# Sample keys of a head pair in one tile, memory weights and mix rows loaded earlier, the memory keys' root on GpSimd

## The chip, the cores and the metric

The kernel runs on one core of a Trainium2 chip. The metric is device time in microseconds of one execution. TensorE (PE in the profile) multiplies and transposes, VectorE (DVE) and ScalarE (ACT) evict, cast and normalize, GpSimd (POOL) does elementwise work on SBUF, and SyncE (SP) issues the DMAs.

## The reference

One layer of a streaming encoder is computed for a prompt of 1024 rows and a sample of 64 rows (width 1024). Both go through an RMS norm, a combined projection to queries, keys and values, and two groups of 8 heads of 64: group A attends in a chunk band with a learned bias, group B causally with a forget gate. Then come the output projection, cross-attention into 256 memory tokens (4 heads of 256), and a gated feed-forward block with a causal convolution of width 3.

What the change touches:

```python
# memory: keys and values of the 256 memory rows
kv = rms_norm(mem, g_mem) @ w_mkv
k = rms_norm(kv[..., :D_MODEL].reshape(b, n, H_M, HEAD_DIM_M), g_mk)
v = kv[..., D_MODEL:].reshape(b, n, H_M, HEAD_DIM_M)
# sample: 64 queries per head against cached keys (A 512, B 1024 rows) and its own 64
k = jnp.concatenate([cache_k, ka], axis=1)
v = jnp.concatenate([cache_v, va], axis=1)
logits = jnp.einsum('bqhd,bkhd->bhqk', q, k) * scale + bias
```

Inputs are fp32, and the outputs also include the new keys and values.

## The kernel before, in words

Every fp32 factor is split into a rounded high part and the remainder (`hi`, `lo`, type fp32r), and a product is the sum of three: high x high, high x low, low x high (`SPLIT`). Where two parts are stacked over the 128 partitions, one matmul does two of them at once.

The program has a phase of projections with the prompt's attention (`Attn`), then the stage around the change, then the output projection (`gemm`, L937), cross-attention and the feed-forward block.

The stage around the change interleaves two kinds of work.

- The memory: 16 units (n, t), n being one of 8 column groups of 256 of `w_mkv` (0 to 3 are keys, 4 to 7 values) and t one of 2 row blocks. A unit is four pieces of six matmuls (`mem_piece`, L679), summed into one of the two buffers of the PSUM bank `pj`. `load_wm` fetches half of a group's weights (512 KB), `split_wm` splits a quarter: ACT casts the high part (L668), GpSimd or DVE subtracts (L669). `mem_end` evicts a unit: for keys the squares' sum (L695), the root of the mean (`rsq`: logarithm and exponential on ACT, three steps on DVE), and the scaled copy `kv` (L698); for values a scaled copy on ACT (L701). `mem_turn` transposes a key unit on PE (L710) and stores it.
- The sample: 8 pairs of heads (`Sample`, in the order `SAMPLES`: four of group B, then four of A). `load` fetches the rows of the pair; `prep` transposes queries and new keys (L754) and splits them into `sq` and `skn`; `splitk` splits the cached keys into `kchi` (ACT, L774) and `kclo` (DVE, L775); `score` multiplies 512 keys at a time (wide products, L797) and the 64 new ones (narrow products, L798), evicts with the running minimum (L800, L802) and takes the exponential on ACT (L808); `turn` transposes the weights (L822) and evicts them as `pth` (ACT) and `ptl` (DVE); `sum` multiplies with the values (L835) and combines the halves (`st` on ACT L842, `su` on DVE L843); `out` transposes (L847) and copies to `smix` (ACT L849).

Before the change each head's keys lie twice in the 128 partitions, against a query tile with the high part above and the low part below, and with zeros in the columns of the other head. So a chunk of 512 keys takes four wide products: two heads, each with `kchi` and `kclo`.

The pieces of the memory are in the list `line`. 15 of them are woven into the last steps of the prompt's attention (`LEFT`), the others into the samples' steps in portions of `PER`. The mix rows (the prompt's attention output, 8 tiles of 128 x 1024) come back from DRAM when `line` is used up: `open_left` loads four, and `split_mix` splits each into `a` (ACT L979, DVE L980); they are the moving operand of the output projection, whose first weights are cast by ACT (L919) and subtracted on GpSimd (L920).

The program gives a list of steps; a scheduler in the framework then sets the order of each engine's queue by its own model of times. Each queue runs in order, so an instruction that waits holds all those behind it.

Of the kernel before, what the change touches and what calls it, by code (L numbers as in the profile page):

```python
# [28 lines left out]
STAGE, MIXES = 4, 8  # L29
# [12 lines left out]
def hybrid_step(ctx: ExitStack, tc: tile.TileContext, i: dict, o: dict):  # L42
# [23 lines left out]
    sqk = dram.tile([8, S, 512], F32, name="sqk")  # L66
# [275 lines left out]
    def proj_sample(p, subs):  # L342
# [22 lines left out]
        def store():  # L365
# [5 lines left out]
            nc.sync.dma_start(sqk[p], qk[:S].rearrange("p h a d -> p (h a d)"))  # L371
# [287 lines left out]
    def load_wm(n, z):  # L659
        raw = mp.tile([P, 4, 256], F32, name="mwraw", bufs=2)  # L660
        nc.sync.dma_start(raw.rearrange("p k c -> p (k c)"), i["w_mkv"][n, z])
        wraw[n, z] = raw

    def split_wm(n, y):
        raw = wraw[n, y // 2][:, 2 * (y % 2):2 * (y % 2) + 2]
        hi = mp.tile([P, 2, 256], F32R, name="mwhi", bufs=6)
        lo = mp.tile([P, 2, 256], F32R, name="mwlo", bufs=6)
# [17 lines left out]
    def mem_end(n, t):  # L685
        pj = mpj.pop((n, t))[:, :256]
        kv = mp.tile([P, 256], F32, name="kv", bufs=2)
# [3 lines left out]
        if n < 4:  # L691
# [4 lines left out]
            dve.tensor_scalar(ms, ms, emem[:, t:t + 1], None, op0=ALU.add)  # L696
            rsq(mp, ms, r, 1)
# [17 lines left out]
    class Sample:  # L715
# [8 lines left out]
        def load(self):  # L724
            p, n = self.p, self.ctx + S
            self.qd = mq.tile([S, 4, P], F32, name="sqd", bufs=2)
            nc.sync.dma_start(self.qd.rearrange("t h d -> t (h d)"), sqk[p])
# [9 lines left out]
            self.kraw, self.craw, self.kc, self.vc = [], [], {}, []  # L737
            for h in range(2):
                raw = mq.tile([P, T], F32, name="kraw", bufs=3)[:, :self.ctx]
                nc.sync.dma_start(raw, self.ck[2 * (p % 4) + h])  # L740
                self.kraw.append(raw)
            for c in range(self.nc):
                raw = mq.tile([P, 4, 2, 64], F32, name="vraw", bufs=3)
                nc.sync.dma_start(raw.rearrange("p k h d -> p (k h d)"), self.cv[p % 4, c])
                self.craw.append(raw)

        def prep(self):
# [5 lines left out]
            for x in range(4):  # L753
                pe.transpose(tq[:, x, :S], self.qd[:, x], ident[:S, :S])  # L754
            self.z = zq[SAMPLES.index(p) % 2]
            self.q = self.z[:, 0:4:3]
            self.kn = [mq.tile([P, 2, S], F32R, name=f"skn{x}", bufs=2) for x in range(2)]
            gained((self.q, self.z[64:, 0:4:3], tq[:, 0:2, :S], gd[:, p // 4, 0:1], LOWER),
                   (self.kn[0], self.kn[1], tq[:, 2:4, :S], gd[:, p // 4, 1:2], ALL))
# [8 lines left out]
        def splitk(self, h):  # L768
            k = self.kraw.pop(0)
            for c in range(self.nc):  # L770
                raw = k[:, c * 512:(c + 1) * 512]
# [4 lines left out]
                self.kc[h, c] = hi, lo  # L776
# [9 lines left out]
        def score(self):  # L786
# [5 lines left out]
            for h in range(2):  # L792
                q = self.z[:, 2 * h:2 * h + 2].rearrange("p h t -> p (h t)")
                for m in range(2):
                    first, last = h + m == 0, h + m == 2
                    for c in range(self.nc):
                        pe.matmul(sp[:, c], q, self.kc[h, c][m], start=first, stop=last)  # L797
                    pe.matmul(sn[:, 0, :S], q, self.kn[m][:, h], start=first, stop=last)  # L798
# [54 lines left out]
    for u, (n, t) in enumerate(units):  # L853
        for c in range(4):
            def piece(n=n, t=t, c=c, u=u):
# [14 lines left out]
    line.append(lambda: mem_turn(*units[-1]))  # L870
# [8 lines left out]
    load_mem(1)  # L879
    split_wm(0, 0)  # L880
# [9 lines left out]
    zq = [mq.tile([P, 4, S], F32R, name=f"sq{x}") for x in range(2)]  # L890
    for x in range(2):
        pool.memset(f32(zq[x][:, 1:3]), 0.0)
    samples = [Sample(p) for p in SAMPLES]
    samples[0].load()
    step(0, [samples[0].prep, lambda: samples[0].splitk(0), lambda: samples[0].splitk(1)])
# [969 lines left out]
```

## Time and profile before

| | us |
|---|---|
| median of 3 runs | 1789.62 (1786.05 to 1790.71) |
| the profiled execution | 1791.44 |
| its span | 1789.7 |
| stage: from the first memory product after the prompt's attention to the first output product | 598.65 to 708.98 |

The times of an engine's instructions count from the span's start. A row of a group gives line, engine, operation, output<-input and count, then busy time and the mean of one in ns, then the engine's idle time ahead of these instructions and what ended it. Matmuls are pipelined: the duration of one is longer than the distance to the next, so what a matmul costs is read from start to start. A wait names the line that waited, and the engine, tile and line that ended the wait.

### The profile page before, as it was taken

What the parts mean: (1) busy time and instruction counts of PE and PEld (TensorE: products, weight loads), DVE (VectorE), ACT (ScalarE), POOL (GpSimd) and SP (SyncE); (2) the same over time, 40 slices, a digit from 0 to 9 for tenths busy, and PEclk for the clock granted to TensorE, in tenths of its full rate; (3) what the DMA queues carried; (4) which work ended last, traced back from release to release, by engine and by line L of the source; (5) the groups of instructions that cost most, each with busy time, mean ns of one, the idle gap of its engine ahead of it and who ended that gap; (6) DMA issues with size and microseconds to landing.
All of it is one profiled execution on the core that took longest, in us unless ns stands there. A gap on an engine that the chain in (4) does not pass through costs nothing.

```text
span 1789.7 us, 33957 instructions
## 1 busy us (share of the span) xinstructions
PE 1717.8 (96%) x12432; PEld 1667.2 (93%) x12432; DVE 1208.6 (68%) x2642; ACT 937.0 (52%) x2058; POOL 644.7 (36%) x931
## 2 busy tenths in 40 slices
PE   7898999999997898999999999999999999999999
PEld 6888999999997787999999999999999999999999
DVE  5767667677677777433444379877777777677994
ACT  6756666677677577334545455433333333433332
POOL 4656657878777443453433612000000000000000
PEclk8999999999999999999999999999999999999999
DMA  7322122122113677441111563222222222884232
GB/s 248 98 63 66 57 73 80 51 73 75 47 56 106 203 248 234 155 144 54 54 48 57 165 204 102 79 76 87 83 87 74 73 73 73 272 296 158 77 118 80
DMA packets 134247, 199.87 MB, mean 112 GB/s; under 512 B 20968, under 2 KB 74088, under 8 KB 134080
## 3 DMA queue, kind: packets, MB, share of 16 engines
q1 hardware_dynamic: 134080, 197.70, 34.9%
q8 instruction: 98, 1.61, 0.4%
q14 instruction: 69, 0.57, 0.1%
HBM read 155.35 MB, written 45.44 MB: 112 GB/s over the span
## 4 chain that ended last, share of the span: by engine, by line
PE 49%; DVE 2%; issue 1%; POOL 1%; DMA 1%; ACT 0%; SPq 0%; POOLq 0%; ACTq 0%; DVEq 0%
PE W L1449 25%; PE W L1746 12%; PE pj L937 7%; PE W L937 1%; PE S L1192 1%; PE tq L1228 1%; PE O L1228 1%; POOL lo L920 1%; DMA kvraw<-in_w_down_dram 1%; PE PT L1215 0%; DMA f<-x2d 0%; PE O L1192 0%; PE PT L1173 0%; POOL s L1207 0%; ACT hi L919 0%
## 5 line engine op out<-in xcount | busy, mean ns | idle before, releaser
L299 PE MATMUL pj<-whi,xhi 128*128 128x384 f32 (+1 forms) x512 | 195.5, 382 | 2.7 <-DVE flog L314 1.6
L299 PE MATMUL pj<-wlo,xhi 128*128 128x384 f32 (+1 forms) x512 | 176.4, 344 | 4.5 <-POOL wlo L123 4.5
L299 PE MATMUL pj<-whi,xlo 128*128 128x384 f32 (+1 forms) x512 | 175.2, 343 | 0.6 <-DVE xlo L131 0.6
L1555 POOL COPY s<-gp 128x2 f32<-128x2 f32 x22 | 15.8, 718 | 335.8 <-DVE gp L1554 335.8
L1449 PE MATMUL W<-h,hi 128*128 128x272 f32 x704 | 134.4, 288 | 1.4 <-ACT qlo L1585 1.4
L504 ACT ACTIVATE s<-s,mx 128x640 f32<-128x640 f32 (+7 forms) x128 | 94.4, 737 | 77.6 <-DVE mx L502 76.7
L1746 PE MATMUL W<-f,hi 128*128 128x272 f32 x672 | 127.6, 287 | 3.6 <-DVE f L1314 2.3
L541 DVE TENSOR_TENSOR ptl<-PT,pth 128x512 fp32r<-128x512 f32 (+2 forms) x192 | 99.5, 522 | 38.5 <-ACT pth L540 36.2
L1449 PEld LDWEIGHTS W<-h,hi 128*128 128x128 f32 x704 | 110.8, 188 | 1.7 <-ACT qlo L1585 1.6
L1746 PEld LDWEIGHTS W<-f,hi 128*128 128x128 f32 x672 | 105.3, 188 | 4.4 <-DVE f L1314 2.5
L540 ACT CAST pth<-PT 128x512 fp32r<-128x512 f32 (+2 forms) x192 | 84.7, 448 | 43.9 <-PE PT L539 42.3
L299 PEld LDWEIGHTS pj<-wlo,xhi 128*128 128x128 f32 x512 | 99.2, 194 | 6.3 <-POOL wlo L123 6.1
L299 PEld LDWEIGHTS pj<-whi,xhi 128*128 128x128 f32 x512 | 98.8, 193 | 4.8 <-DVE flog L314 1.9
L1449 PE MATMUL W<-h,lo 128*128 128x272 f32 x352 | 101.8, 289 | 0.0
L1313 ACT CAST hi<-raw 128x512 fp32r<-128x512 f32 x68 | 42.2, 621 | 109.5 <-PE W L1449 59.2
L299 PEld LDWEIGHTS pj<-whi,xlo 128*128 128x128 f32 x512 | 97.6, 191 | 1.8 <-DVE xlo L131 1.6
L539 PE MATMUL PT<-ident,s 128*128 128x128 f32 x528 | 90.6, 278 | 7.8 <-DVE ptl L541 7.3
L1746 PE MATMUL W<-f,lo 128*128 128x272 f32 x336 | 96.7, 288 | 0.0
L499 PE MATMUL S<-kh,q 128*128 128x256 f32 (+1 forms) x304 | 77.6, 280 | 12.2 <-DVE mx L502 12.0
L937 PE MATMUL pj<-a,hi 128*128 128x384 f32 (+1 forms) x352 | 88.8, 335 | 0.2 <-ACT hi L919 0.2
L507 POOL TENSOR_SCALAR s<-s,ssum 128x640 f32<-128x640 f32 (+6 forms) x96 | 70.3, 734 | 48.6 <-DVE ssum L505 36.5
L554 PE MATMUL O<-pth,v 128*128 128x256 f32 (+1 forms) x304 | 78.1, 281 | 8.3 <-ACT mhi L265 7.6
(551 smaller groups left out, 6038.1 us busy)
## 6 DMA issues: line engine op xcount, KB each, us to landing
raw<-in_w_down_dram SPq DMA_DIRECT2D x45, 256.0 KB, 3.6
wraw<-in_w_dram SPq DMA_DIRECT2D x56, 192.0 KB, 2.4
raw<-in_w_up_dram SPq DMA_DIRECT2D x41, 256.0 KB, 2.8
h<-ad SPq DMA_DIRECT2D x32, 272.0 KB, 5.0
mwraw<-in_w_mkv_dram SPq DMA_DIRECT2D x16, 512.0 KB, 5.9
raw<-in_w_mo_dram SPq DMA_DIRECT2D x32, 256.0 KB, 3.4
kvraw<-in_w_down_dram SPq DMA_DIRECT2D x32, 256.0 KB, 3.2
ad<-t SPq DMA_DIRECT2D x22, 272.0 KB, 2.3
```

The costliest lines, as they stand in the source:

```text
L299: pe.matmul(pj[:, :nw], x2[a][:, k, t * P:(t + 1) * P], wt[k][b][:, :nw], start=n == 0, stop=n == 3 * KT - 1)
L499: pe.matmul(sp[:, a:a + (k1 - k0) * P], q, kk[:, h, src], start=m == 0, stop=m == 1)
L504: act.activation(s[:, :n], s[:, :n], ACT.Exp, bias=mx, scale=-1.0, accum_out=sm)
L507: pool.tensor_scalar(s[:, :n], s[:, :n], sm, 1.0, op0=ALU.mult, op1=ALU.mult)
L539: pe.transpose(pt[:, b - ch[0]], self.s[j][:, (b - w0) * P:(b - w0 + 1) * P], ident)
L540: act.copy(hi[:, f:f + n, j], pt[:, f:f + n])
L541: dve.tensor_tensor(lo[:, f:f + n, j], pt[:, f:f + n], f32(hi[:, f:f + n, j]), op=ALU.subtract)
L554: pe.matmul(op[:, cols], groups[p, b // 2].v[:, b % 2, h].rearrange("p a d -> p (a d)"), pt[:, x, cols], start=b == self.full[0] and m == ...
L937: pe.matmul(out()[:, :cn], w[a][:, k % 4], x[b][k][:, c0:c0 + cn], start=k == 0 and n == 0, stop=k == KT - 1 and n == 2)
L1313: act.copy(hi, t)
L1449: pe.matmul(w[:, z, :Q], a(p, j), rights[j][b][:, z * Q:z * Q + Q], start=fresh and begin and j == 0 and x == 0, stop=final and end and j ...
L1746: pe.matmul(ws[m][:, z, :Q], la[p][:, m * P:(m + 1) * P], ra[b][:, z * Q:z * Q + Q], start=first and y == 0 and what in opening, stop=fina ...
```

## The change

Cached keys: the two heads of a pair now share one tile, head 0 in partitions 0 to 63 and head 1 in 64 to 127, each loaded once. The query tile `z` holds, for the high and for the low part, a block for each head with zeros elsewhere. One product serves both heads, and three (high x high, high x low, low x high) do what four did. Only one copy of the sample's queries and new keys is stored and transposed.

Memory: weights have four buffers in place of two, are fetched two groups ahead, and a group is split half a unit earlier. The keys' root is taken on GpSimd (an add and a power of -0.5) in place of ACT and DVE. A key unit is transposed during the second unit after it, where it was the next one; `kv` has three buffers.

Mix rows: four of the eight are loaded beside samples 4 and 5 (`MIXED`), two at the start of the output projection's stage into the buffers of `kraw`, and two after the first two are split.

```diff
-STAGE, MIXES = 4, 8
+MIXED, MIXES = (4, 5), 8
...
     def load_wm(n, z):
-        raw = mp.tile([P, 4, 256], F32, name="mwraw", bufs=2)
+        raw = mp.tile([P, 4, 256], F32, name="mwraw", bufs=4)
...
             act.activation(sq, pj, ACT.Square, scale=1.0 / 16, accum_out=ms)
-            dve.tensor_scalar(ms, ms, emem[:, t:t + 1], None, op0=ALU.add)
-            rsq(mp, ms, r, 1)
+            pool.tensor_scalar(ms, ms, emem[:, t:t + 1], 1.0, op0=ALU.add, op1=ALU.mult)
+            pool.tensor_tensor(r, ms, mhalf[:, 0:1], op=ALU.pow)
...
-            self.kraw, self.craw, self.kc, self.vc = [], [], {}, []
+            self.craw, self.kc, self.vc = [], [], []
+            self.kraw = mq.tile([P, T], F32, name="kraw", bufs=2)[:, :self.ctx]
             for h in range(2):
-                raw = mq.tile([P, T], F32, name="kraw", bufs=3)[:, :self.ctx]
-                nc.sync.dma_start(raw, self.ck[2 * (p % 4) + h])
-                self.kraw.append(raw)
+                nc.sync.dma_start(self.kraw[h * 64:(h + 1) * 64], self.ck[2 * (p % 4) + h][0:64])
...
-            for x in range(4):
+            for x in range(2):
                 pe.transpose(tq[:, x, :S], self.qd[:, x], ident[:S, :S])
...
-            for h in range(2):
-                q = self.z[:, 2 * h:2 * h + 2].rearrange("p h t -> p (h t)")
-                for m in range(2):
-                    first, last = h + m == 0, h + m == 2
-                    for c in range(self.nc):
-                        pe.matmul(sp[:, c], q, self.kc[h, c][m], start=first, stop=last)
-                    pe.matmul(sn[:, 0, :S], q, self.kn[m][:, h], start=first, stop=last)
+            for m, (x, y) in enumerate(SPLIT):
+                q = self.z[:, x].rearrange("p h t -> p (h t)")
+                for c in range(self.nc):
+                    pe.matmul(sp[:, c], q, self.kc[c][y], start=m == 0, stop=m == 2)
+                pe.matmul(sn[:, 0, :S], q, self.kn[y], start=m == 0, stop=m == 2)
...
-                if n < 7:
-                    if t == 0 and c in (1, 2):
-                        load_wm(n + 1, c - 1)
-                    if t == 1:
-                        split_wm(n + 1, c)
+                if n < 6 and t == 0 and c in (1, 2):
+                    load_wm(n + 2, c - 1)
+                if n < 7 and 2 <= 4 * t + c < 6:
+                    split_wm(n + 1, 4 * t + c - 2)
                 mem_piece(n, t, c)
-                if c == 2 and u:
-                    mem_turn(*units[u - 1])
+                if c == 1 and u > 1:
+                    mem_turn(*units[u - 2])
...
+    mraws = []
+
+    def load_mix(tag="mraw"):
+        k = len(mraws)
+        mraws.append(mq.tile([P, T], F32, name=tag, bufs={"mraw": 4, "kraw": 2}[tag]))
+        nc.sync.dma_start(mraws[k], mixd[k])
...
+        if x in MIXED:
+            load_mix()
+            load_mix()
```

The change moves instructions in every queue of the stage. Two places matter most. The first is GpSimd's queue where the first memory units end: `s` (L762, L765) is the bias of a sample, `mwlo` the low part of memory weights, `mms` and `mr` the mean square and the root of a unit, `sq` the clearing of query tiles. Before:

```order
L762 TENSOR_SCALAR s<-s,stok 128x1088
L765 AFFINE_SELECT s<-s 64x64 x2
L762 TENSOR_SCALAR s<-s,stok 128x1088
L669 TENSOR_TENSOR mwlo<-mwraw,mwhi 128x512
L892 MEMSET sq_9094 128x128
```

The same place after:

```order
L696 TENSOR_SCALAR mms<-mms,emem 128x1
L697 TENSOR_TENSOR mr<-mms,mhalf 128x1
L669 TENSOR_TENSOR mwlo<-mwraw,mwhi 128x512
L762 TENSOR_SCALAR s<-s,stok 128x1088
L669 TENSOR_TENSOR mwlo<-mwraw,mwhi 128x512
L889 MEMSET sq_9078 128x256
L696 TENSOR_SCALAR mms<-mms,emem 128x1
L889 MEMSET sq_9079 128x256
L697 TENSOR_TENSOR mr<-mms,mhalf 128x1
```

Between the root of unit 0 and that of unit 1 there now stand two weight splits, a bias and two clears.

The second place is ACT's queue at the stage's end. Before, from the last sample's key cast to the cast of the first output weights (`hi`):

```order
L774 CAST kchi<-kraw 128x512
L823 CAST pth<-PT 64x128
L782 CAST vc<-vraw 128x8x64
L979 CAST a_10467<-mraw 128x1024
L808 ACTIVATE s,ssum<-s,mx 128x576
L842 ACTIVATE st<-O,ssum 64x64
L979 CAST a_10468<-mraw 128x1024
L842 ACTIVATE st<-O,ssum 64x64
L979 CAST a_10469<-mraw 128x1024
L979 CAST a_10470<-mraw 128x1024
L849 COPY smix<-PT 64x64 x2
L919 CAST hi<-raw 128x512 x3
```

After, from the copy of the last memory unit (`kv`) through sample 6 to sample 7 (counted from 0 in the order of `SAMPLES`):

```order
L701 ACTIVATE kv<-pj,rmem 128x256
L773 CAST kchi<-kraw 128x512
L846 COPY smix<-PT 64x64 x2
L781 CAST vc<-vraw 128x8x64
L805 ACTIVATE s,ssum<-s,mx 128x576
L820 CAST pth<-PT 128x4x128
L820 CAST pth<-PT 64x128
L265 ACTIVATE sq_9079<-tq,gd 64x64 x2
L839 ACTIVATE st<-O,ssum 64x64
L265 ACTIVATE skn_10312<-tq,gd 128x64
L839 ACTIVATE st<-O,ssum 64x64
L846 COPY smix<-PT 64x64 x2
```

and directly behind it:

```order
L773 CAST kchi<-kraw 128x512
L781 CAST vc<-vraw 128x8x64
L805 ACTIVATE s,ssum<-s,mx 128x576
L977 CAST a_10350<-mraw 128x1024
L977 CAST a_10351<-mraw 128x1024
L977 CAST a_10352<-mraw 128x1024
L977 CAST a_10353<-mraw 128x1024
L977 CAST a_10354<-kraw 128x1024
L977 CAST a_10355<-kraw 128x1024
L923 CAST hi<-raw 128x512 x3
```

Where three mix casts and sample 6's output stood between the last exponential and the first weight cast, six mix casts stand now; and sample 6's keys are now cast behind the last memory unit, where before they were cast ahead of it.

More of the change, by code (lines that the diff above doesn't have):

```diff
@@ L889, in hybrid_step @@
     smix = mq.tile([P, 8, S], F32, name="smix")
[L890 removed]
+    zq = [mq.tile([P, 2, 2, S], F32R, name=f"sq{x}") for x in range(2)]
     for x in range(2):
[L892 removed]
+        pool.memset(f32(zq[x]), 0.0)
+    mraws = []
[3 more added lines that the diff above has]
+        nc.sync.dma_start(mraws[k], mixd[k])
     samples = [Sample(p) for p in SAMPLES]
     samples[0].load()
[L895 removed]
+    step(0, [samples[0].prep, samples[0].splitk])
     late_left, mixes = ExitStack(), ExitStack()
@@ L968, in open_left @@
         ha = mixes.enter_context(tc.tile_pool(name="ha", bufs=1, side="left"))
[L969 removed]
         mixr.extend(parts(ha, "a"))
         stream.fetch()
[L972 to L976 removed]
         def split_mix(k):
[L979 to L990 removed]
+            act.copy(mixr[0][k][:, 0:T], mraws[k])
+            dve.tensor_tensor(mixr[1][k][:, 0:T], mraws[k], f32(mixr[0][k][:, 0:T]), op=ALU.subtract)
+            if len(mraws) < KT:
+                load_mix()
+        for k in range(2):
+            load_mix("kraw")
+        return ha, [lambda k=k: split_mix(k) for k in range(KT)], x
     old, mixes_todo, ha = [], [], None
```

54 lines of the change are left out of this document (21 added, 33 removed).

## The prediction

> **What bounds the kernel now.** I read the page first: where the span goes by engine.
>
> ```profile
> PE 1717.8 (96%) x12432; PEld 1667.2 (93%) x12432; DVE 1208.6 (68%) x2642; ACT 937.0 (52%) x2058; POOL 644.7 (36%) x931
> ```
>
> That row is an average, and everything changed lies in one short stage: the memory's keys and values interleaved with the sample attention. So next I read the busy time by stretch of just that stage. A row is start:end, length, then busy us of PE, PEld, DVE, ACT and POOL, then granted clock, DMA share and GB/s. The three first stretches run from the first memory product after the prompt's attention to sample 0's transposes, then to the last memory product, then to the first output product; the fourth is what follows.
>
> ```profile
> 598.65:626.50 27.85, 23.70 (x182) 21.92 (x180) 19.34 (x48) 12.86 (x37) 12.50 (x18) 1.00 0.66 208
> 626.50:698.17 71.67, 68.06 (x475) 58.85 (x475) 52.09 (x131) 52.30 (x130) 30.05 (x25) 1.00 0.76 236
> 698.17:708.98 10.81, 6.15 (x32) 4.05 (x31) 8.49 (x18) 9.66 (x21) 1.45 (x1) 0.94 0.75 241
> 708.98:720.00 11.02, 10.36 (x44) 9.22 (x45) 9.29 (x14) 7.72 (x18) 6.28 (x4) 0.75 0.62 212
> ```
>
> Over the first three, PE is idle 4.1 + 3.6 + 4.7 = 12.4 us out of 110.3. PE is what the stage waits for in its first 99.5 us; in the last 10.8 us ACT (9.66 of 10.81) and DVE are fuller than PE. The order of PE after this stage is the same in both programs, so a shift of the first output product passes on to the end. The waits of PE (total, times, longest), in the stretches up to and after 698.17, say who holds it:
>
> ```profile
> PE PT L710 <- DVE kv L698: 3.8, 4, 1.3
> PE pj L679 <- POOL mwlo L669: 1.1, 2, 0.6
> ...
> PE PT L847 <- DVE su L843: 4.4, 2, 4.0
> ```
>
> So 3.8 us wait for the memory's normalized keys, 1.1 for split weights, and 4.0 sit in one hole at the end, ahead of the last sample's transposes.
>
> **The change part by part.** *Three products.* The timeline of PE (start, duration, line) gives the real price, which is start to start, since matmuls overlap:
>
> ```profile
> 613.74 0.43 PE L754 MATMUL tq<-ident,sqd 64*128 64x64 f32 x4
> 614.11 0.38 PE L679 MATMUL pj<-mwhi,mhi 128*128 128x256 f32 x1
> ...
> 618.08 0.60 PE L798 MATMUL tq<-skn,sq 128*128 128x64 f32 x4
> 618.52 0.36 PE L679 MATMUL pj<-mwlo,mhi 128*128 128x256 f32 x1
> ...
> 618.84 0.39 PE L797 MATMUL S<-kchi,sq 128*128 128x512 f32 x1
> 619.07 0.28 PE L679 MATMUL pj<-mwhi,mhi 128*128 128x256 f32 x1
> 619.19 0.28 PE L679 MATMUL pj<-mwlo,mhi 128*128 128x256 f32 x1
> ...
> 697.89 0.28 PE L679 MATMUL pj<-mwhi,mlo 128*128 128x256 f32 x1
> ...
> 708.98 1.01 PE L937 MATMUL pj<-a,hi 128*128 128x384 f32 x2 [0.22 <-ACT hi L919]
> ```
>
> A wide score product takes 0.23 us, a narrow one 0.44/4 = 0.11, a transpose 0.37/4 = 0.09, a memory product 0.12. Removed in all: 12 wide (48 to 36), 8 narrow, 16 transposes = 2.8 + 0.9 + 1.4 = 5.1 us of PE. Ahead of the last memory product it is a little more, since the queue now puts sample 6's scores and sample 7's transposes behind it: 14 x 0.23 + 7 x 0.11 + 18 x 0.09 = **-5.6**. Halved key loads and splits free DMA, ACT and DVE, which are not the bound there: 0.
>
> *The root on GpSimd.* PE's transposes of the keys move six memory pieces further back, so their 3.8 us go. What is late next is the bank: there are two `pj`, so unit u+2 cannot open until DVE has evicted unit u. These GpSimd groups (mean ns after the busy time) price the new path; the root of one column has no row, so I bound it by 0.28 (the add) below and 1.09 (a four-column pow) above and take 1.05, the same operation.
>
> ```profile
> L669 POOL TENSOR_TENSOR mwlo<-mwraw,mwhi 128x512 fp32r<-128x512 f32 x16 | 21.9, 1368 | 12.6 <-ACT mwhi L668 9.1 <-ACT rsq_y L77 3.4
> L762 POOL TENSOR_SCALAR s<-s,stok 128x1088 f32<-128x1088 f32 x4 | 5.1, 1284 | 4.6 <-DMA s<-negs 4.6
> ...
> L245 POOL TENSOR_TENSOR r<-m,mhalf 128x4 f32<-128x4 f32 x32 | 34.9, 1090 | 2.3
> L244 POOL TENSOR_SCALAR m<-m,eps 128x4 f32<-128x4 f32 x32 | 9.0, 282 | 61.0 <-DVE m L241 61.0
> ```
>
> In the new queue, unit 1's add and root stand behind two weight splits and one bias add after unit 0's: 2 x 1.37 + 1.28 + about 0.4 of clears, then 0.28 + 1.05 = 5.75 us later than unit 0's. Units end 24 x 0.12 = 2.86 us apart, and unit 0's keys come about 0.4 before their bank is wanted, so unit 3 waits 5.75 - 2.86 - 0.4, about 2.4. Later units have samples between them and meet no such heap. Net 2.4 - 3.8 = **-1.4**; bounds: -3.8 (nobody waits) and +3.4 (three such waits).
>
> *Weights two groups ahead.* The 1.1 us wait goes: **-1.1**. But all four splits of group 1 now fall into the tail of the prompt's attention, where PE waits for evictions on ACT and DVE anyway, one of them ahead of a reciprocal on DVE, two on GpSimd ahead of both normalizations of `s`. The GpSimd row above prices one at 1.37 us. Bounds 0 and 2 x 1.37; I take **+1.0**.
>
> *The end.* Here the order decides. Before, sample 6's scores were multiplied ahead of the last memory product (697.89 + 0.28), and 10.8 us later came the first output product. Now sample 6's key cast stands on ACT behind the last memory unit's `kv` copy, and sample 7's stands behind sample 6's output: two samples in series, and the six casts of mix rows follow the second one's exponential. Groups of ACT and DVE (mean ns after busy):
>
> ```profile
> L774 ACT CAST kchi<-kraw 128x512 fp32r<-128x512 f32 x24 | 14.1, 614 | 2.2 <-DMA kraw<-in_cbk_dram 2.0
> L979 ACT CAST a<-mraw 128x1024 fp32r<-128x1024 f32 x8 | 8.3, 1046 | 0.3 <-DMA mraw<-mixd 0.3
> ...
> L823 ACT CAST pth<-PT 128x512 fp32r<-128x512 f32 x12 | 6.8, 581 | 2.8 <-PE PT L822 2.8
> L842 ACT ACTIVATE st<-O,ssum 64x64 f32<-64x64 f32 x16 | 4.9, 308 | 6.0 <-PE O L835 5.3 <-DVE su L843 0.5
> ...
> L701 ACT ACTIVATE kv<-pj,rmem 128x256 f32<-128x256 f32 x8 | 3.8, 474 | 3.1 <-PE pj L679 2.5 <-ACT pth L823 0.5
> L808 ACT ACTIVATE s<-s,mx 128x576 f32<-128x576 f32 x4 | 3.1, 777 | 4.8 <-DVE mx L807 4.8
> ...
> L849 ACT COPY smix<-PT 64x64 f32<-64x64 f32 x14 | 2.8, 203 | 1.0 <-PE PT L847 0.7
> L919 ACT CAST hi<-raw 128x512 fp32r<-128x512 f32 x4 | 2.3, 616 | 0.0
> ...
> L808 ACT ACTIVATION_READ_ACCUMULATOR s<-s,mx 128x1 f32 x8 | 1.5, 186 | 0.0
> ```
>
> ```profile
> L775 DVE TENSOR_TENSOR kclo<-kraw,kchi 128x512 fp32r<-128x512 f32 x24 | 16.7, 721 | 2.6 <-ACT kchi L774 2.5
> ...
> L824 DVE TENSOR_TENSOR ptl<-PT,pth 128x512 fp32r<-128x512 f32 x12 | 8.2, 687 | 2.2 <-ACT pth L823 2.0
> ...
> L843 DVE SCALAR_TENSOR_TENSOR su<-O,ssum,st 64x64 f32<-64x64 f32 x16 | 4.5, 281 | 1.4 <-ACT st L842 1.0
> ...
> L800 DVE CUSTOM_DVE_ANT_0 s<-S,s 128x512 f32<-128x512 f32 x4 | 2.8, 689 | 2.3 <-PE tq L798 1.2 <-PE S L797 1.1
> ```
>
> Along the chain: `kv` 0.47, then cast 0.61, difference 0.72, the last two score products about 0.7, eviction 0.69, maximum about 0.3, exponential 0.78 + 0.19: 4.5. Transposes 0.5, two evictions 0.58 + 0.69, ten value products about 1.5: 3.3. Two rounds of 0.31 + 0.28 for the output, a query cast of about 0.35 between them, its transpose 0.25, two copies 0.41: 2.2. Sample 7 from its key cast to its exponential: 4.0. Six mix casts 6 x 1.05 and the weight's cast 0.62: 6.9. Sum 20.9, where 10.8 stood: **+10.1**. The mix rows do arrive early, but their casts cannot start early, so that part costs or saves nothing here. Bounds: 0, if the chain is as short as before's, and +13 if each of some fifteen hand-overs costs 0.2 us.
>
> *The clock.* Rows of 2 us where PE waits again and again (columns as above):
>
> ```profile
> 588.00:590.00 2.00, 0.66 (x4) 0.47 (x4) 1.94 (x4) 0.60 (x2) 0.00 (x0) 1.00 0.20 66
> 590.00:592.00 2.00, 0.92 (x6) 0.92 (x7) 1.66 (x6) 2.00 (x4) 0.06 (x1) 0.89 0.98 293
> 592.00:594.00 2.00, 2.00 (x11) 2.00 (x11) 0.69 (x1) 1.04 (x2) 1.05 (x1) 0.50 1.04 265
> ```
>
> After 4 us at 40% busy the granted clock was 0.50, though PE worked in between. The new end has about 6 us of PE work in 20.9, so its second half runs at half clock: some ten products of 0.12 us double: **+1.0** (bounds 0 and 3). The output products start at 0.50 as they do now (fourth stretch, 0.75 on average); I add **+0.5** for a last eviction that now queues behind seven mix differences on DVE. The Trainium skill (TensorE: Matmul & The Clock Gate, Part 1: The HAM clock gate) has the clock fall after an idle window of about 3.4 us. By that rule read as one idle stretch, no wait before the last is long enough, and the sum would be 1.0 lower. The row above speaks for the shorter trigger.
>
> Sum: -5.6 - 1.4 - 1.1 + 1.0 + 10.1 + 1.0 + 0.5 = **+4.5 us**. The profiled execution took 1791.44 us (span 1789.7 and 1.7 around it), so it would take 1795.9. It was 1.8 above the median of the three runs, 1789.62, so I forecast **1794** for the median. 0.3%, 5.4 us, is about what a measurement of this kernel can tell from no change (its three runs spread over 4.7). The forecast lies within, on the slow side.
>
> **The rivals.** *Faster: the end is covered.* If the two last samples overlap with memory products as they do now, the +10.1, +1.0 and +0.5 fall away: -7.1, 1782.5. For it: PE is 95% busy in the second stretch, so memory products last long. Against: ACT's queue has `kv` ahead of sample 6's keys, and nothing overtakes in a queue.
>
> *Slower: GpSimd holds the banks.* Its place is unit 2 to unit 7: each root waits behind splits of weights and of sample values, and each of those waits for an ACT cast. It decides from where a root comes more than 2.86 us after its unit's end. At 2.4 us for each of four units, +7.2 on top: 1801. For it: GpSimd's rows show 12.6 us of waiting ahead of its splits. Against: from unit 4 on, score and value products stand between units and give time. The Trainium skill (SBUF — State Buffer, the list of which ops grab the shared pair) has a DVE `tensor_tensor` with both inputs in SBUF and a GpSimd op lock each other out. If all eight adds and roots held DVE on the path, an estimate would be 8 x 1.37, or 11 us more. No row here shows that price for so small an op.
>
> *Nothing: waits only change their names.* The stage keeps its 12.4 us of PE waits, split otherwise, and the 5.1 us of products are lost to slower clock and the attention's tail: 1790.
>
> **How the numbers follow.** Forecast 0.50 (its own range 1788 to 1800: 0.31 within 0.3%, 0.19 above it); covered end 0.16 (0.12 faster, 0.04 the same); GpSimd 0.20 (0.19 slower, 0.01 the same); nothing 0.14 (0.13 the same, 0.01 slower). So faster 0.12, same 0.49, slower 0.39. Range 1785 to 1801: the forecast with its bounds, all of the last case, and the near half of each of the two others.
>
> **What would show it.** The score products in the profile after: 36 wide ones and 24 narrow. The wait of PE's transposes for `kv` gone, and one wait of 2 to 3 us of a memory product for `kv`'s bank near the third or fourth unit. The last memory product 6 to 8 us earlier than 697.89, and yet the first output product at about 713, with 14 to 16 us of idle PE between them: waits for the exponential twice, for `su`, and one of 5 to 6 us for the weight's cast behind six mix casts. A granted clock of 0.5 over the second half of that stretch. It would be wrong if the first output product came less than 14 us after the last memory product, or if PE waited over 6 us for `kv` in all.

## The result, and the profile after

The changed kernel takes 1799.99 us (median of 4 runs, 1798.16 to 1800.25) against 1788.15 us before on the same chip: a ratio of 1.0062, 95% interval 1.0050 to 1.0074. It is slower, the side on which the forecast of 1794 leaned: by 11.8 us in the medians and by 8.8 us in the two profiled executions (spans 1798.5 and 1789.7), where 4.5 was forecast. The profiled execution before, 1791.44 us, lies above all four timed runs of that kernel, so the profiles show less of the loss than the medians do.

The busy time by stretch of the changed kernel, from the first memory product to the last, from there to the first output product, and 15 us more (columns as in the prediction: start:end, length, busy PE, PEld, DVE, ACT, POOL, granted clock, DMA share, GB/s):

```profile
598.76:692.70 93.94, 85.71 (x617) 77.50 (x616) 58.89 (x134) 55.95 (x139) 48.69 (x59) 0.98 0.73 211
692.70:716.05 23.35, 10.93 (x37) 6.63 (x35) 11.50 (x26) 13.61 (x28) 3.00 (x3) 0.60 0.41 136
716.05:731.05 15.00, 13.55 (x63) 12.03 (x64) 11.43 (x21) 8.09 (x22) 8.35 (x5) 0.83 0.40 126
```

The last memory product comes 5.2 us earlier (692.70 against 697.89), the first output product 7.1 us later (716.05 against 708.98). Between them lie 23.1 us where 10.8 lay. The granted clock there is 0.60, and 0.98, not 1.00, ahead of it.

The waits of PE in the changed kernel (total, times, longest), first from 598.3 to 693.2, then from there to 730:

```profile
PE tq L795 <- DVE skn L266: 2.9, 4, 1.1
PE S L794 <- DVE kclo L774: 2.7, 3, 1.1
PE pj L679 <- DVE kv L698: 1.6, 1, 1.6
...
PE pj L941 <- ACT hi L923: 4.9, 1, 4.9
PE PT L819 <- ACT s L805: 3.8, 2, 1.9
```

The waits for keys at the transposes (3.8) and for split weights (1.1) are gone; waits for the new keys' split (`skn`) and the cached keys' low part (`kclo`), 5.6 us, have taken their place. The end shows the chain that the prediction named: two waits for an exponential, and 4.9 us for the weight's cast.

The timeline of that end (start, duration, engine, line):

```profile
692.70 0.28 PE L679 MATMUL pj<-mwhi,mlo 128*128 128x256 f32 x1
...
696.48 0.77 ACT L805 ACTIVATE s<-s,mx 128x576 f32<-128x576 f32 x1 [1.52 <-DVE mx L804]
...
705.36 0.62 ACT L773 CAST kchi<-kraw 128x512 fp32r<-128x512 f32 x1
...
708.94 0.78 ACT L805 ACTIVATE s<-s,mx 128x576 f32<-128x576 f32 x1 [2.44 <-DVE mx L804]
...
709.71 3.87 ACT L977 CAST a<-mraw 128x1024 fp32r<-128x1024 f32 x4
...
713.49 1.99 ACT L977 CAST a<-kraw 128x1024 fp32r<-128x1024 f32 x2
...
715.38 1.66 ACT L923 CAST hi<-raw 128x512 fp32r<-128x512 f32 x3
```

Before, sample 7's key cast and exponential stood here:

```profile
699.27 0.62 ACT L774 CAST kchi<-kraw 128x512 fp32r<-128x512 f32 x1
...
703.48 0.78 ACT L808 ACTIVATE s<-s,mx 128x576 f32<-128x576 f32 x1 [0.96 <-DVE mx L807]
```

Sample 6's exponential is hardly later than before (696.48 against 695.85). Sample 7's is: 708.94 against 703.48, because its keys are cast at 705.36, behind all of sample 6. The keys themselves had long arrived: their load was issued at 688.8, and the loads into that tile land within 3.6 us. Then six mix casts run without a gap, and the weight's cast behind them.

To compare kernels I cut each stage into stretches of 1 us and took from the rows the length less PE's busy time (idle) and the busy time times one minus the granted clock (what the lower clock cost PE, an estimate: only where PE is what the rest waits for does it show in the time). Each row below is one profiled execution; "ahead" runs from the first memory product to the end of the last, "end" from there to the first output product; all in us.

| kernel | ahead: length, idle, clock | end: length, idle, clock |
|---|---|---|
| before | 99.5, 7.8, 0.0 | 10.8, 4.7, 0.6 |
| changed | 94.2, 8.2, 1.7 | 23.1, 12.4, 4.5 |

So ahead of the last memory product the change took 7.5 us of PE work away and gave back 0.5 as idle time and 1.7 as clock. In the end it added 7.7 idle and 4.0 clock. What follows the first output product is 1.7 us longer (1.2 of it in the output product, up to the next stage's first product). What comes behind the output product is the same program in all the kernels here, and in their profiles it took between 974.9 and 979.0 us; so a microsecond or two between single profiles says nothing.

### The profile page after: what moved, and what is told of

The parts are those of the page before. It is cut to its first block, busy times and chain, and to the rows that moved or that the text cites. A ratio compares the mean times of both kernels' runs of the same rounds, so it can differ in the third digit from the quotient of the medians.

```text
span 1798.5 us, 33844 instructions
## 1 busy us (share of the span) xinstructions
PE 1717.4 (95%) x12396; PEld 1666.1 (93%) x12396; DVE 1197.8 (67%) x2606; ACT 931.7 (52%) x2038; POOL 656.4 (36%) x947
## 4 chain that ended last, share of the span: by engine, by line
PE 71%; DVE 10%; ACT 6%; DMA 5%; issue 4%; POOL 4%; SPq 0%; POOLq 0%; DVEq 0%; ACTq 0%
PE W L1447 25%; PE pj L941 11%; PE pj L299 11%; PE W L1744 9%; PE O L554 3%; PE PT L539 2%; PE S L499 2%; ACT s L504 1%; PE pj L679 1%; DVE s L502 1%; PE tq L326 1%; DMA s<-in_xn_dram 1%; PE S L1190 1%; PE tq L1226 1%; PE O L1226 1%
## 5 line engine op out<-in xcount | busy, mean ns | idle before, releaser
L499 PE MATMUL S<-kh,q 128*128 128x256 f32 (+1 forms) x304 | 77.7, 280 | 12.1 <-DVE mx L502 12.0
```

Source lines behind the costliest of these rows:

```text
L499: pe.matmul(sp[:, a:a + (k1 - k0) * P], q, kk[:, h, src], start=m == 0, stop=m == 1)
```

## The experiments

Times are medians; the ratio is to the kernel before, which ran beside each (its medians there were 1788.1 to 1789.5 us). Line numbers differ by a few between these kernels.

**The changed kernel without its mix rows.** The rows are staged as before (the lines that open their stage on the left are not shown).

```
-MIXED, MIXES = (4, 5), 8
+MIXED, MIXES = (), 8
...
-        for k in range(2):
-            load_mix("kraw")
+        for k in range(4):
+            load_mix()
```

> The changed kernel with the mix rows as before: a stage of four tiles on the left, opened when the memory's tiles are closed, all eight rows loaded there; the three products, the root on GpSimd and the weights two groups ahead stay. Theory: the mix rows beside the samples are what moved the two last samples behind each other. Without them sample 6's scores stand ahead of the last memory product again and sample 7's key cast stands ahead of sample 6's output, so the first output product comes 11 to 14 us after the last memory product instead of 23.1, at 705 to 709 us, and the time is 1784 to 1789, 11 to 16 below the changed kernel's 1800. Rival one: shorter memory work by itself uncovers the samples, whatever the mix rows do; the idle stretch stays over 18 us and the time at 1797 to 1801. Rival two: GpSimd's root and early splits cost it; also 1797 to 1801, with new waits ahead of the last memory product.

1790.94 us, 1.0018 (1.0008 to 1.0029): 9 us of the loss are gone. (Its twelve runs spread from 1788.9 to 1796.2; the profiled one took 1789.43.) Its stretches from the first memory product:

```profile
596.85:693.02 96.17, 87.00 (x622) 78.03 (x621) 59.66 (x139) 57.12 (x142) 51.16 (x61) 0.98 0.64 186
693.02:705.13 12.11, 6.34 (x33) 4.22 (x31) 7.63 (x20) 9.94 (x26) 1.53 (x1) 0.86 0.80 273
```

The end is 11.8 us long and its clock costs 0.9. So shorter memory work by itself does not uncover the samples. The time is 2 us above the range that I gave, and that is left for the other parts.

**The three products alone.** The root, the weights and the mix rows are as before; only the keys' tile and the products are changed.

> Only the keys of a pair in one tile with three products; the root, the weights and the mix rows as before. Theory: the last memory product comes about 5 us before the 697.89 of before, minus 0 to 3 us of waits for the new splits of queries and keys (seen as 4.0 for skn and 2.7 for kclo in the changed kernel), so at 693 to 696; 11 to 14 us later the first output product, at 705 to 709; time 1784 to 1788, within 2 us of the first run of this set. Rival one (shorter memory work uncovers the samples): the idle stretch grows by what the memory gained and the time is that of before, 1788 to 1790, or worse. Rival two (GpSimd's root and the early splits cost time): this one is 3 us or more faster than the first run of this set.

1799.69 us, 1.0061 (1.0050 to 1.0073): as slow as the whole change, with fewer edits. Theory and rivals all missed this (one rival allowed for "or worse", by a longer end, but not for this): the last memory product comes at 699.32, later than before's, with 4.5 us less PE work by the 1 us rows. Ahead it has 12.1 us of idle time and 3.4 of clock; the end is 14.2 us, with 3.2 of clock. Two-microsecond rows of it:

```profile
632.00:634.00 2.00, 0.11 (x1) 0.11 (x2) 1.93 (x5) 0.85 (x3) 1.26 (x1) 1.00 0.16 46
634.00:636.00 2.00, 2.00 (x8) 1.55 (x8) 0.68 (x2) 0.00 (x0) 0.00 (x0) 0.53 0.52 125
636.00:638.00 2.00, 2.00 (x8) 1.55 (x8) 0.69 (x4) 0.72 (x3) 0.20 (x1) 0.50 0.94 356
638.00:640.00 2.00, 2.00 (x12) 1.98 (x11) 0.49 (x2) 0.64 (x3) 0.25 (x1) 0.50 0.28 113
```

PE stands almost still from 632 to 634 (a memory product waits 1.9 us for `kv`), and then works for nearly 7 us at half clock. The timeline shows why `kv` is late; `rsq_a` and `mr` are steps of the root, one column each:

```profile
630.06 1.81 POOL L782 TENSOR_TENSOR vc<-vraw,vc 128x512 fp32r<-128x512 f32 x1
...
630.64 1.25 DVE L78 TENSOR_TENSOR rsq_a<-mms,rsq_y 128x1 f32<-128x1 f32 x1
...
632.03 1.26 POOL L669 TENSOR_TENSOR mwlo<-mwraw,mwhi 128x512 fp32r<-128x512 f32 x1 [0.16 <-ACT mwhi L668]
632.12 1.20 DVE L80 SCALAR_TENSOR_TENSOR mr<-rsq_a,rsq_y 128x1 f32<-128x1 f32 x1
...
633.89 0.39 PE L679 MATMUL pj<-mwhi,mhi 128*128 128x256 f32 x1 [1.89 <-DVE kv L698]
```

The step between these two (L79) starts while GpSimd is idle and takes 0.16 us. The two that run beside an instruction of GpSimd take 1.25 and 1.20, and each ends within 0.03 us of that instruction's end. So the root is 2.1 us late for two small steps, PE waits, and the clock falls. The loss ahead can be made without GpSimd's root.

**The weight's cast ahead of the mix rows.** In the changed kernel the first output weights are cast first, and rows 4 and 5 wait for the ring of the others.

```
         stream.fetch()
+        stream.upto(4)
...
-        for k in range(2):
-            load_mix("kraw")
```

> The changed kernel, but the first output weights are cast ahead of the mix rows in the program, and mix rows 4 and 5 are loaded into the ring of the other rows once it comes free, so that no load on the queue waits for the last sample's keys ahead of the weights. Theory: the hole of 4.9 us ahead of the first output product shrinks by about three mix casts (3 x 1.04 us) less one weight cast (0.62): 2.0 to 3.0 us, time 1797 to 1798.5; the two samples in series stay (sample 7's exponential 12 to 13 us behind sample 6's), so most of the loss stays. Rival (the hole at the end is nearly all of the loss): 1793 to 1795. Rival (something ahead of the last memory product): 1800, unchanged.

1804.93 us, 1.0085 (1.0072 to 1.0098): 5 us slower still. The end did shrink by 2.8 us, to 20.2. But the last two mix rows were now cast as late as this:

```profile
727.61 1.05 ACT L978 CAST a<-mraw 128x1024 fp32r<-128x1024 f32 x1
728.70 1.05 ACT L978 CAST a<-mraw 128x1024 fp32r<-128x1024 f32 x1
```

In the changed kernel they are cast by 719.4. The output product, which needs all eight, then ran 8 us longer than there. The run moved the hole instead of closing it, and since it makes two edits at once it says little about the hole's price.

**The root on ACT and DVE.** The changed kernel with two lines as before:

```
-            pool.tensor_scalar(ms, ms, emem[:, t:t + 1], 1.0, op0=ALU.add, op1=ALU.mult)
-            pool.tensor_tensor(r, ms, mhalf[:, 0:1], op=ALU.pow)
+            dve.tensor_scalar(ms, ms, emem[:, t:t + 1], None, op0=ALU.add)
+            rsq(mp, ms, r, 1)
```

> The changed kernel with the keys' root on ACT and DVE as before (logarithm, exponential and a correction step), the transposes of the keys still two units back. Theory: the end is the same chain of two samples, and the wait for the bank near unit 3 (1.6 us) is small, so 1798 to 1801. Rival (GpSimd holds the banks): 1793 to 1797, with the last memory product 3 us or more earlier than 692.7.

1794.89 us, 1.0036 (1.0023 to 1.0048): the root on GpSimd costs 5 us, as the rival said. The last memory product ends 92.6 us behind the start of the first one, against 94.2, and the end is 21.2 us long, against 23.1; together 3.5 us. (The first memory product comes 2.3 us earlier as well, but no root stands ahead of it, and its place varies from 596.5 to 599.6 over the profiles here.) The reason is not the bank alone. DVE's groups in the changed kernel, from 598 to 693 (mean ns after busy, then the idle time before them):

```profile
L669 DVE TENSOR_TENSOR mwlo<-mwraw,mwhi 128x512 fp32r<-128x512 f32 x12 | 14.5, 1214 | 1.2 <-ACT mwhi L668 1.1
L774 DVE TENSOR_TENSOR kclo<-kraw,kchi 128x512 fp32r<-128x512 f32 x10 | 9.6, 995 | 1.2 <-ACT kchi L773 1.2
...
L698 DVE SCALAR_TENSOR_TENSOR kv<-pj,mr,gmk 128x256 f32<-128x256 f32 x8 | 3.9, 484 | 12.6 <-POOL mr L697 12.6
```

The same two groups with the root as before:

```profile
L774 DVE TENSOR_TENSOR kclo<-kraw,kchi 128x512 fp32r<-128x512 f32 x11 | 7.6, 722 | 0.9 <-ACT kchi L773 0.7 <-DMA s<-rows 0.2
L698 DVE SCALAR_TENSOR_TENSOR kv<-pj,mr,gmk 128x256 f32<-128x256 f32 x8 | 3.8, 477 | 0.1
```

With GpSimd's root, `kv` stands at the head of DVE's queue and waits 12.6 us in all, and everything behind it waits too. And a difference for the cached keys takes 995 ns instead of 722. What each of these is worth by itself is not shown.

**The root and the mix rows as before.** Three products and the weights two groups ahead stay.

> The changed kernel with the root on ACT and DVE and the mix rows both as before: three products, weights two groups ahead and the later transposes stay. Undoing the root took 5 us from the changed kernel (1794.9 against 1800.0) and undoing the mix rows 9 (1790.9). Theory: the two act in different places (the root holds DVE's queue ahead of the last memory product, the mix rows set the end), so they add: 1784 to 1788, below the 1789 of before. Rival: the root only cost because the end was uncovered: 1790 to 1792, as without the mix rows.

1788.05 us, 0.9995 (0.9986 to 1.0003): the upper end of the range, and not the rival's 1790 to 1792. The two nearly add: together their undoing takes back 12 us, a little less than 9 + 5. What remains of the change is worth nothing measurable in the time. Yet in the one profile the stage is shorter than before (first memory product to first output product 104.2 us against 110.3). Of that, 1.3 us are lost in the output product (105.0 against 103.7); the rest lies ahead of the stage and behind the output product, within the scatter of these profiles.

**The mix rows alone**, on the kernel before:

> The kernel before with the mix rows beside the samples and nothing else of the change. Theory: two loads of 512 KB each between the loads of the last samples are enough to set sample 7 behind sample 6, whatever the memory's work is: 18 to 23 us from the last memory product to the first output product instead of 10.8, and a time of 1796 to 1800. Rival: it is the shorter memory work that uncovers the samples, and here it is not shorter: 11 to 13 us, 1788 to 1791.

1792.74 us, 1.0023 (1.0011 to 1.0035): slower by 4, half of what I expected. The end is 18.0 us long against 10.8, and the same hole is in it:

```profile
PE pj L944 <- ACT hi L926: 4.9, 1, 4.9
PE PT L822 <- ACT s L808: 1.9, 1, 1.9
```

The sample order does turn on the mix rows, with the memory's work the same. But where I had expected only a loss, the last memory product ends 2.8 us sooner behind the first (96.8 us against 99.5; PE has 1.9 us less to do there and 0.9 less idle time), and the longer end gives 7.2 back. The difference, 4.4, is about what the time shows.

**The mix rows loaded two samples later** in the changed kernel:

```
-MIXED, MIXES = (4, 5), 8
+MIXED, MIXES = (6, 7), 8
```

> The changed kernel with its mix rows still beside the samples, but the four early ones loaded two samples later (behind all loads of the samples). Theory: it is the place of these loads in the order that counts; the two last samples overlap again, 11 to 15 us from the last memory product to the first output product, 1789 to 1793. Rival: rows in the cached keys' ring and six casts in a row cost it wherever the loads stand: 18 us or more and 1796 to 1801.

1792.97 us, 1.0024 (1.0015 to 1.0033): one pair of numbers takes 7 us of the loss away. The end is 14.3 us, with a hole of 2.4 us for the weight's cast. Sample 7's keys are again cast (696.09) ahead of sample 6's output (699.08). So most of the price is not that the rows lie beside the samples; it is the place of four loads in the program, with which the two last samples come to stand one behind the other in ACT's queue. What is left, 2 us against the version without mix rows, is within the error of the two.

**The weights two groups ahead alone**, with the later transposes, on the kernel before:

> The kernel before with the memory's weights two groups ahead and its transposes two units back, and nothing else. By the prediction's own terms: the waits for keys (3.8 us) and split weights (1.1) go, the attention's tail may lose 1.0, so 1784 to 1787. Rival: the end is set by the chain of samples and not by the memory's work, so what is saved ahead of the last memory product comes back behind it: 1788 to 1791, with a longer stretch from the last memory product to the first output product.

1793.58 us, 1.0026 (1.0016 to 1.0036): slower, and not where the rival looked for it. The end is 10.3 us, shorter than before. The loss lies ahead, where the last memory product ends 103.4 us behind the start of the first (99.5 before), with 9.8 idle and 5.1 of clock; two of three falls of the clock are seen here:

```profile
616.00:618.00 2.00, 0.26 (x3) 0.06 (x1) 2.00 (x4) 0.98 (x3) 1.02 (x1) 1.00 0.44 115
618.00:620.00 2.00, 1.82 (x11) 1.86 (x12) 1.90 (x7) 1.42 (x4) 0.46 (x1) 0.68 0.84 289
620.00:622.00 2.00, 2.00 (x11) 1.90 (x10) 1.05 (x3) 1.31 (x4) 0.00 (x0) 0.50 0.88 294
...
626.00:628.00 2.00, 0.81 (x3) 0.48 (x3) 1.97 (x3) 0.00 (x0) 1.10 (x1) 1.00 0.62 167
628.00:630.00 2.00, 2.00 (x14) 1.81 (x13) 1.54 (x6) 1.31 (x2) 0.46 (x1) 0.74 0.77 115
630.00:632.00 2.00, 2.00 (x12) 2.00 (x11) 1.37 (x4) 2.00 (x6) 0.00 (x0) 0.50 0.90 328
```

In both stalls DVE is full (2.00 and 1.97 of 2.00 us), and one-column steps of the root again stand beside GpSimd: two of 1.13 and 1.22 us ahead of the first stall's `kv`, one of 1.22 us ahead of the second's, each ending with GpSimd's instruction.

**Filling the end.** The changed kernel with products that nothing needs:

```
-WARM = 20
+WARM, PADS = 20, 60
...
+        if x == 7:
+            pad = bank("pj")
+            main = [lambda k=k: pe.matmul(pad[:, :384], mixpad[0], mixpad[1][:, :384], start=True, stop=True) for k in range(PADS)]
```

> The changed kernel with 60 products of zeros (128x384, into a bank that is free there) put between the last memory product and the first output product; they go into PE's waits, the other instructions keep their order but for one cast of a mix row. They add work that nothing needs. Theory: in this stretch PE ran at 0.59 of its clock because it waited again and again, which cost about 4 us of the 23; with the waits filled the clock stays near 1.0 there and for the first output products, and the time falls by 2.5 to 5 us, to 1795 to 1797.5. Rival: ACT and DVE set this stretch and PE's clock costs nothing, or the fillers stand in the way: 1799 to 1803.

1796.13 us, 1.0046 (1.0033 to 1.0059): 3 to 4 us faster than the changed kernel for 60 products more. The two intervals overlap, and one of its five runs (1799.33) is as slow as that kernel, so the times alone do not settle it; the profile is clearer. Its end, and 15 us more:

```profile
692.05:712.50 20.45, 16.47 (x97) 14.22 (x95) 11.68 (x26) 13.62 (x28) 3.04 (x3) 1.00 0.51 171
712.50:727.50 15.00, 13.31 (x64) 11.96 (x65) 11.14 (x21) 8.09 (x22) 8.13 (x5) 0.89 0.39 118
```

The clock stays at 1.00, and the same chain takes 20.2 us instead of 23.1. So the low clock had a price of about 3 us in the end itself.

**All splits of the memory's weights on DVE**, on the version of 1788.05 us:

```
-        (dve if y % 2 else pool).tensor_tensor(lo, raw, f32(hi), op=ALU.subtract)
+        dve.tensor_tensor(lo, raw, f32(hi), op=ALU.subtract)
```

> Three products, weights two groups ahead, root and mix rows as before (1788.05), and all of the memory weights' low parts on DVE, none on GpSimd. Theory: side by side the two engines slow each other (DVE's split takes 0.88 to 1.2 us beside GpSimd's and 0.69 alone), so DVE does all 24 in little more time than it took for its 12, GpSimd's 16 us go, and fewer waits stand ahead of the last memory product: 1784 to 1787. Rival: DVE is full (75 to 90% busy from 616 to 646 us) and becomes the bound: 1790 to 1794.

1782.79 us, 0.9973 (0.9963 to 0.9983): faster than both kernels. Its DVE groups and stretches:

```profile
L669 DVE TENSOR_TENSOR mwlo<-mwraw,mwhi 128x512 fp32r<-128x512 f32 x24 | 18.6, 790 | 2.3 <-ACT mwhi L668 2.3
L774 DVE TENSOR_TENSOR kclo<-kraw,kchi 128x512 fp32r<-128x512 f32 x12 | 8.2, 689 | 2.7 <-ACT kchi L773 2.0 <-DMA kraw<-in_cak_dram 0.6
```

```profile
598.19:688.44 90.25, 84.77 (x623) 76.53 (x621) 66.41 (x185) 59.52 (x160) 27.46 (x33) 1.00 0.70 200
688.44:699.14 10.70, 5.58 (x32) 3.92 (x30) 7.96 (x18) 9.52 (x21) 1.30 (x1) 0.90 0.79 269
```

DVE does 24 splits in 18.6 us; in the version of 1788.05 us it took 14.4 for 12. The clock never falls ahead of the last memory product, and PE's idle time there is 5.5 us. The rival's full DVE did not become the bound.

**The same with the root on GpSimd:**

> Mix rows as before, the root on GpSimd (1790.9), and all low parts of the memory's weights on DVE. Theory: the root is late because it stands behind splits in GpSimd's queue, and DVE, which waits 14.4 us for it, is held; without the splits that wait falls below 7 us and the time is 1785 to 1789, near the version with the root as before. Rival: the wait comes from the root's own two steps (0.30 and 0.56 us) and the hand-overs: no change, 1789 to 1793.

1786.81 us, 0.9996 (0.9988 to 1.0005), against 1790.94 with the splits shared. DVE's wait for the root is shorter, but not below 7:

```profile
DVE kv L698 <- POOL mr L697: 8.5, 7, 2.9
```

It is still 4 us above the last version, though its last memory product ends 2 us closer to the first one (88.4 us against 90.5): its end is 15.1 us, with 3.2 of clock. What the root costs can move from one side of the last memory product to the other.

**The same splits on the kernel before:**

> The kernel before, with all low parts of the memory's weights on DVE and nothing of the change. Moving them took the version with three products and the weights ahead from 1788.05 to 1782.8. Theory: DVE had room for them there because the change halves the splits of cached keys (24 to 12, at 0.72 us about 8.6 us less on DVE); before, DVE is 83 to 94% busy from 618 to 658 us, so 13 more splits of 0.69 to 0.8 us there are not hidden: 1788 to 1793. Rival: the gain is only that the two engines no longer slow each other, and the change has no part in it: 1782 to 1785.

1787.24 us, 0.9989 (0.9977 to 1.0000): about 2 us, with an interval that reaches 1.0000, between theory and rival. The splits get faster here too (711 ns for 26 of them, against 884 shared), and DVE carries them. So of the 5 us that the best version gains over before, this edit alone gives about 2. The other 3 or so came with the three products and the early weights beside it; the intervals of the two versions (up to 0.9983, and from 0.9977) just overlap.

## Why the prediction was right and wrong

*The direction and the range held; the size did not.* The sum was +4.5, the profiled executions differ by +8.8, the medians by 11.8. By places, forecast and profile: ahead of the first memory product +1.0 and +0.1; from there to the end of the last -8.1 and -5.3; the end with its clock +11.1 and +12.3; behind it +0.5 and +1.7. That 1800 still lies within 1785 to 1801 owes something to the width of that range. It is also close to the 1801 of the rival "GpSimd holds the banks", by luck: of that rival's four waits for a bank one came, and the loss lies elsewhere.

*Products, -5.6.* Right as far as PE's work goes: 36 wide products and 24 narrow ones are there, and PE has 7.5 us less work ahead of the last memory product. But as an edit by itself it lost 10 us. The step that failed is "halved key loads and splits free DMA, ACT and DVE, which are not the bound there: 0": in the stall of that run DVE is busy 1.93 of 2.00 us and PE 0.11. Removing work from PE only shortens the stage if what feeds PE keeps its pace, and it removes the cover of the remaining waits.

*Root, -1.4.* The wait was foreseen at its place and nearly in size (1.6 us on the bank where 2.4 stood, the transposes' 3.8 us gone). The term was still of the wrong sign: undoing it gains 3 to 5 us in three pairs of versions. I priced the bank and left out what stands behind `kv` in DVE's queue. The rival "GpSimd holds the banks" had the engine right; its mechanism was too narrow.

*Weights, -1.1, and the attention's tail, +1.0.* The wait for split weights went. The tail cost nothing visible: the first memory product starts at 598.76 against 598.65 (a scatter of 3 us over the profiles here hides a term of 1). Not foreseen: the splits now fall together. In the changed kernel's timeline, around 638 us:

```profile
638.20 1.28 POOL L782 TENSOR_TENSOR vc<-vraw,vc 128x512 fp32r<-128x512 f32 x1 [0.81 <-ACT vc L781]
...
638.42 3.28 DVE L774 TENSOR_TENSOR kclo<-kraw,kchi 128x512 fp32r<-128x512 f32 x2
...
639.66 1.50 POOL L669 TENSOR_TENSOR mwlo<-mwraw,mwhi 128x512 fp32r<-128x512 f32 x1 [0.18 <-ACT mwhi L668]
640.08 0.50 PE L794 MATMUL S<-kclo,sq 128*128 128x512 f32 x1 [1.10 <-DVE kclo L774]
```

Two differences on DVE take 3.28 us beside two of GpSimd's; at the end, with GpSimd idle, one takes 0.69. PE waits 1.1 us for the first. The Trainium skill (SBUF — State Buffer, "Who interferes with whom") says that a DVE `tensor_tensor` with both inputs in SBUF and a GpSimd operation that reads SBUF exclude each other for a whole instruction. These rows agree, and so do the one-column steps in the run with the three products alone, and the runs with all splits on one engine. The prediction named this rule beside a rival, but applied it to the small adds and roots on GpSimd, where it gave 11 us, and not to the splits. It said that no row shows such a price for so small an operation. For DVE's side the trace before has one: at 604.26 a one-column step of the root (L78) takes 1.25 us beside a split on GpSimd that ends at 605.50, where the next step takes 0.16.

*The end, +10.1.* The chain came as it was laid out: 23.1 us where 20.9 and 1.0 for the clock were forecast, and 20.2 us with the clock kept at 1.00 by the 60 products. Its cause is the mix rows' place among the loads; the prediction ascribed it to the queues' order without asking which edit had set it.

*The clock, +1.0.* This is the term that was most mis-sized. In the end the estimate from the rows is 4.0 us more than before, and the filled end shows about 3 us of it as a real price: the clock was low from about 697 on, most of the stretch and not only its second half. Ahead of the last memory product another 1.7 us, an estimate too, were not in the sum at all; these rows of the changed kernel show them:

```profile
636.00:638.00 2.00, 1.01 (x8) 1.01 (x9) 1.48 (x4) 2.00 (x5) 1.19 (x3) 1.00 0.97 327
638.00:640.00 2.00, 0.98 (x7) 0.66 (x5) 2.00 (x3) 1.22 (x3) 1.62 (x2) 1.00 1.06 245
640.00:642.00 2.00, 1.09 (x5) 0.84 (x6) 2.00 (x5) 0.00 (x0) 1.16 (x1) 1.00 1.03 214
642.00:644.00 2.00, 2.00 (x10) 1.82 (x10) 1.66 (x4) 0.00 (x0) 0.00 (x0) 0.64 1.01 187
644.00:646.00 2.00, 2.00 (x12) 2.00 (x11) 0.59 (x5) 1.29 (x2) 0.00 (x0) 0.51 0.51 166
```

After 6 us in which PE is half busy, no wait longer than 1.1 us, it runs at half clock for about 3.4 us. It comes just behind the stall of the slow `kclo`.

*After, +0.5.* 1.7 was measured, 1.2 of it in the output product.

Summed: between the first and the last memory product -8.1 was forecast and -5.3 came. PE's work fell by 1.9 more than forecast. Against that stand the clock (1.7) and an idle time that rose by 0.5 where 2.5 less was forecast, for the waits for `skn` and `kclo` that nobody had listed.

*What stays open.* Why the scheduler sets the last two samples in series when two loads precede theirs; its model is not in the trace. And why the three products alone, or the early weights alone, cost 4 to 10 us while both together cost nothing. The profiles show where (idle time and clock ahead of the last memory product) and what stands at the stalls (steps of the root on DVE beside GpSimd's instructions). But every edit also reorders all queues, and with it which instructions of the two engines meet; so prices of single edits do not add here.

## What to carry to other kernels

When an edit removes work from the fullest engine, price next what its remaining waits uncover, and look at the granted clock in short rows: a stretch of some microseconds in which PE is half busy or less can cost a second time, at half clock, as in the rows of three kernels here. When a small step moves to another engine, count everything that queues behind the instruction that waits for it, and whether its new neighbours read the same memory as the work that they are to run beside. And where a scheduler orders the queues, vary the place of a load by itself before giving up the idea: here one pair of numbers was worth 7 us.

## What was not expected of the hardware

- The clock fell without any long wait. In the changed kernel 6 us at 50% busy were enough, with waits of at most 1.1 us; the fall lasted about 3.4 us and cost 1.7, and the three falls with the early weights alone 5.1 together. The Trainium skill (TensorE: Matmul & The Clock Gate, Part 1: The HAM clock gate) lets the clock fall after an idle window of about 3.4 us and rise after a busy one. The length of the half clock agrees; the fall does not, if the window has to be idle throughout.
- Work that nothing needs can pay: with 60 products of zeros the end took 20.2 us in place of 23.1, and the kernel 3 to 4 us less.
- A step of one column on DVE, 0.16 us alone, takes up to 1.25 us beside an instruction of GpSimd: it lasts until that one ends.
- Sharing the splits between DVE and GpSimd gave next to nothing: 14.4 us of DVE for 12 of 24 in the version of 1788.05 us, 18.6 us for all 24 in the best one.
- A root of one column on GpSimd takes 0.56 us (L697 in the changed kernel: 8 of them, mean 558 ns), half of what the prediction took from the four-column one.
